# A three-block transformer kernel: unnormalised entry of layer 1, one pass for both norms between the blocks, a shorter gate series, values behind the first scores, elementwise work moved from GpSimd to VectorE

## The chip, the cores and the metric

One core of one Trainium2 chip runs the whole program. The metric is the device time of an execution in microseconds. Engines: TensorE (PE, with PEld for its weight loads), VectorE (DVE), ScalarE (ACT), GpSimd (POOL), SyncE (SP, which issues nearly all DMAs).

## The reference, cut to what matters

Two models in a row on 256 latent tokens of width 1024, each beside a context stream of 256 tokens; float32 throughout. Block 1 is an mLSTM with window attention and a convolutional feed-forward. The second model has layer 0 (retention and a state-space mixer) and layer 1 (latent attention with 16 heads), each with a gated feed-forward.

```
x = first_block(...)                                   # ends with rmsnorm(x, final_norm)
for i in range(2):                                     # second_block: h_lat starts as x, h_ctx is its own context
    a_ctx = rms_norm(h_ctx) * (1 + m_ctx[1]) + m_ctx[0]
    a_lat = rms_norm(h_lat) * (1 + m_lat[1]) + m_lat[0]
    o_ctx, o_lat = retention_ssd_mixer(...) if i == 0 else mla_mixer(...)
    h_lat = h_lat + m_lat[2] * o_lat
    h_lat = h_lat + m_lat[5] * swiglu(rms_norm(h_lat) * (1 + m_lat[4]) + m_lat[3])
    ...                                                # h_ctx the same way, in layer 0 only
return rms_norm(h_lat, final_norm_w)

# mla_mixer: c_q, c_kv, k_pe = split(h @ w_in)   (768, 256, 32 columns)
#   q = rms_norm(c_q) @ w_uq;  k_nope, v = split(rms_norm(c_kv) @ w_ukv)
#   keys and values of context and latent together, softmax over 512 keys, then w_out
# gates: log_sigmoid and softplus, both through log1p(exp(-|x|))
```

The m vectors are products of a conditioning vector with the modulation matrices w_ada.

## The kernel before, in words

Activations lie feature-major: 8 tiles of 128 features by 256 tokens (`xs` latent, `cs` context). Each float32 matmul is three passes (`mm3`, L283 to L287) over a rounded high half and a low half of both operands. `load_w` (L259) brings weights by DMA into tag `wr`, rounds them on ScalarE into `wh` (L270), and takes the low half `wl` by a subtraction (L273). The rule `PW` (L30) puts that subtraction on GpSimd for lane `f` and, in layer 0's latent pass, for the second half of each load of lane `m`; elsewhere on VectorE. A lane is a set of buffers: `m` (main) has 5 PSUM banks and 3 raw weight buffers, `f` (fill) 2 banks and 2 raw buffers, `a` (side) one bank; `L.on(other)` borrows another lane's banks.

The program is written as Python generators, woven with `weave`. The order in which they issue is only a priority: the whole program is one list, scheduled by the tile framework with its own model of times, and `soon()` raises a part's priority. Each engine then runs its instructions in the fixed order which that schedule gave.

Order of the work: modulation and norms; block 1 (projections, gates, mLSTM, window attention, output projection, feed-forward woven with `ada_dve`, which forms modulation columns on VectorE, L417); `final_norm` (L826), which normalises `xs`; layer 0 (`l0_stream`) first for the context on lane `f` up to its states, then for the latents on lane `m`, which begins with a norm of its own (L1124); the feed-forward of both streams, 512 columns wide, woven with more `ada_dve`; layer 1 (`l1`, L1567); the last feed-forward; the last norm.

Two forms of a norm exist. `norm_mod` (L501) squares on ScalarE (`sumsq`), adds on VectorE, sums over features by matmuls with ones (L463), takes the power -1/2 on GpSimd (L229), spreads the result over partitions by a matmul with the identity (L472), and then scales each block on VectorE (L516) and splits it into halves; odd blocks take the low half on GpSimd (L519, L523). The raw form (`raw_mod`, L476) writes unnormalised blocks with two extra columns for the shift as each block of an output projection is finished; matmuls run on 258 columns, and `raw_fix` (L492) applies 1/rms to the result. Before the change only layer 1's feed-forward uses the raw form.

In layer 1, `kv(0)` projects the context to keys and rope part, `kv(1)` the latents, then come 6 query blocks (`ev_q`); `nq` is the norm of the queries, woven with `l1_keys` (keys) and two `proj_tm` (`values`); then the query projection `wuq`, then `attend`, which issues the scores and softmax of 3 heads ahead (`AH1`). In `softmax` (L1008) the first half of the probabilities is scaled on VectorE (L1031), the second on GpSimd (L1032). Further GpSimd work: the first product of `rope` (L577), low halves of the feed-forward activations (L627, L678), and in layer 0 small gated sums (L1318, L1347, L1368, L1387, L1426 to L1428), which the change leaves there.

```
def load_w(self, L, src, n, unit):
    raw = self.tile([P, 1024], F32, "wr" + L.w.name, L.raw)
    nc.sync.dma_start(raw[:, :n], src)
...
    nc.scalar.copy(hi[:, :c1 - c0], raw[:, c0:c1])
    eng = nc.gpsimd if PW(self, L, len(subs)) else nc.vector
    eng.tensor_sub(lo[:, :c1 - c0], raw[:, c0:c1], hi[:, :c1 - c0])
```

## Time and profile before

| | |
|---|---|
| median of 3 runs | 1576.56 us (1572.23 to 1579.45) |
| profiled execution | 1574.25 us, of it 1572.5 us span |
| instructions | 28299, of them 10518 matmuls |
| mean granted TensorE clock | 0.977 of full speed |
| HBM read | 265.60 MB |

The span is what the profile shows between its first and last instruction; the profiled execution is 1.75 us longer. Matmul records are pipelined and their ends modelled, so a busy TensorE can still run below its pace; the number of matmuls in a stretch tells more. A clock of 1.00 is 2.4 GHz, the lower level 0.50 is 1.2 GHz, and a value between is a mean over the stretch. VectorE's busy time holds whatever an instruction spends waiting for memory.

### The profile page before, as it was taken

The numbers are of one execution on the slowest core, as the hardware profiler recorded it, in microseconds if no ns is written. First come the engines' busy times: TensorE is split into PE (matmuls) and PEld (weight loads), VectorE is DVE, ScalarE is ACT, GpSimd is POOL, SyncE is SP. The second block draws the span as 40 slices with busy tenths as digits, with TensorE's granted clock in tenths as the row PEclk, the third lists the DMA queues.
The fourth block names the chain that finished last, engine by engine and source line by source line (L and its number), as shares of the span: only waits on it lengthen the run. The fifth ranks groups of instructions, "written<-read, shape, count | busy, mean of one in ns | idle before, by whom it ended". The sixth has DMA issues, their size and how long they took to land.

```text
span 1572.5 us, 28299 instructions
## 1 busy us (share of the span) xinstructions
PE 1500.6 (95%) x10518; PEld 1328.4 (84%) x10518; DVE 1141.5 (73%) x2369; ACT 789.3 (50%) x1703; POOL 397.4 (25%) x373
## 2 busy tenths in 40 slices
PE   5899999999999997999899999999998999999997
PEld 3598877889999977889899888888898865899997
DVE  4457588589999946777775347988686776687776
ACT  3444547575545455644474323322355556566563
POOL 0102136143222254466572101101011112010000
PEclk9799999999999998999999999999999999999999
DMA  9855651347777763424255225688533340255553
GB/s 335 275 183 202 230 186 41 134 175 237 255 251 240 243 209 121 130 91 148 69 168 167 95 88 207 208 290 275 179 122 109 101 139 1 95 175 177 185 181 115
DMA packets 81387, 268.50 MB, mean 171 GB/s; under 512 B 9056, under 2 KB 10720, under 8 KB 80992
## 3 DMA queue, kind: packets, MB, share of 16 engines
q1 hardware_dynamic: 80672, 266.16, 50.7%
q8 instruction: 82, 1.34, 0.3%
q10 hardware_dynamic: 576, 0.52, 0.1%
q14 instruction: 57, 0.47, 0.1%
HBM read 265.60 MB, written 1.05 MB: 170 GB/s over the span
## 4 chain that ended last, share of the span: by engine, by line
PE 82%; DVE 9%; issue 4%; DMA 3%; ACT 1%; POOL 0%; SPq 0%; POOLq 0%; DVEq 0%; ACTq 0%
PE t_ppm L285 18%; PE t_ppm L287 18%; PE t_ppm L286 18%; PE t_ppf L285 4%; PE t_ppf L286 4%; PE t_ppf L287 4%; DVE t_wlm L273 2%; DMA t_wra<-in_wada 2%; PE t_ppm L1649 2%; PE t_ppa L427 2%; PE t_ppm L1050 1%; PE t_ppf L1064 1%; PE t_ppm L972 1%; PE t_ppm L1082 1%; DVE t_junk L417 1%
## 5 line engine op out<-in xcount | busy, mean ns | idle before, releaser
L270 ACT CAST t_whm<-t_wrm 128x512 fp32r<-128x512 f32 (+2 forms) x588 | 346.3, 598 | 402.6 <-PE t_ppm L286 281.8
L273 DVE TENSOR_TENSOR t_wlm<-t_wrm,t_whm 128x512 fp32r<-128x512 f32 (+3 forms) x551 | 406.0, 743 | 151.7 <-ACT t_whm L270 140.7
L285 PE MATMUL t_ppm<-t_g1m,t_whm 128*128 128x256 f32 x952 | 271.8, 290 | 1.3 <-ACT t_g1m L522 0.8
L287 PE MATMUL t_ppm<-t_g1m,t_wlm 128*128 128x256 f32 x952 | 268.7, 287 | 3.3 <-DVE t_wlm L273 3.2
L286 PE MATMUL t_ppm<-t_g1m,t_whm 128*128 128x256 f32 x952 | 269.7, 286 | 0.0
L287 PEld LDWEIGHTS t_ppm<-t_g1m,t_wlm 128*128 128x128 f32 x952 | 181.9, 192 | 7.5 <-DVE t_wlm L273 5.1
L285 PEld LDWEIGHTS t_ppm<-t_g1m,t_whm 128*128 128x128 f32 x952 | 182.0, 193 | 5.9 <-issue 3.1
L286 PEld LDWEIGHTS t_ppm<-t_g1m,t_whm 128*128 128x128 f32 x952 | 183.0, 193 | 2.0 <-issue 1.7
L273 POOL TENSOR_TENSOR t_wlf<-t_wrf,t_whf 128x512 fp32r<-128x512 f32 (+1 forms) x92 | 121.4, 1333 | 168.5 <-ACT t_whf L270 150.3
L286 PE MATMUL t_ppm<-t_h8m,t_whm 128*128 128x512 f32 (+2 forms) x448 | 159.7, 357 | 1.9 <-DVE t_h8m L525 1.9
L285 PE MATMUL t_ppm<-t_h8m,t_whm 128*128 128x512 f32 (+1 forms) x448 | 158.5, 357 | 2.7 <-ACT t_h8m L524 2.7
L417 DVE SCALAR_TENSOR_TENSOR t_junk<-t_wra,t_sc 128x1024 bf16<-128x1024 f32 x120 | 148.7, 1243 | 16.8 <-DMA t_wra<-in_wada 16.0
L287 PE MATMUL t_ppm<-t_h8m,t_wlm 128*128 128x512 f32 (+2 forms) x448 | 159.5, 357 | 0.0
L270 ACT CAST t_whf<-t_wrf 128x512 fp32r<-128x512 f32 (+2 forms) x148 | 82.9, 573 | 99.9 <-PE t_ppf L286 70.6
L286 PE MATMUL t_ppm<-t_part,t_whm 128*128 128x258 f32 (+1 forms) x400 | 114.1, 285 | 0.0
L287 PE MATMUL t_ppm<-t_part,t_wlm 128*128 128x258 f32 (+1 forms) x400 | 113.8, 285 | 0.0
L285 PE MATMUL t_ppm<-t_part,t_whm 128*128 128x258 f32 (+1 forms) x400 | 113.4, 284 | 0.0
L287 PE MATMUL t_ppm<-t_g2m,t_wlm 128*128 128x256 f32 x352 | 98.9, 284 | 0.6 <-DVE t_wlm L273 0.5
L285 PE MATMUL t_ppm<-t_g2m,t_whm 128*128 128x256 f32 x352 | 99.1, 283 | 0.0
L286 PE MATMUL t_ppm<-t_g2m,t_whm 128*128 128x256 f32 x352 | 99.1, 282 | 0.0
L286 PEld LDWEIGHTS t_ppm<-t_h8m,t_whm 128*128 128x128 f32 (+1 forms) x448 | 84.0, 187 | 15.3 <-DVE t_h8m L525 2.3
L285 PEld LDWEIGHTS t_ppm<-t_h8m,t_whm 128*128 128x128 f32 x448 | 83.1, 187 | 16.3 <-ACT t_h8m L524 2.9
(541 smaller groups left out, 3518.3 us busy)
## 6 DMA issues: line engine op xcount, KB each, us to landing
t_wrm<-in_wup SPq DMA_DIRECT2D x132, 512.0 KB, 3.7
t_wra<-in_wada SPq DMA_DIRECT2D x102, 512.0 KB, 4.9
t_wrm<-in_w_fm SPq DMA_DIRECT2D x30, 512.0 KB, 3.6
t_wra<-in_wada20t SPq DMA_DIRECT2D x24, 512.0 KB, 4.4
t_wrf<-in_w_fm SPq DMA_DIRECT2D x20, 512.0 KB, 4.5
t_wrf<-in_wd SPq DMA_DIRECT2D x24, 384.0 KB, 3.8
t_wrm<-in_win_fm SPq DMA_DIRECT2D x17, 512.0 KB, 3.6
t_wrm<-in_wdown SPq DMA_DIRECT2D x16, 512.0 KB, 4.6
```

The lines of the kernel that those rows point to most:

```text
L270: nc.scalar.copy(hi[:, :c1 - c0], raw[:, c0:c1])
L273: eng.tensor_sub(lo[:, :c1 - c0], raw[:, c0:c1], hi[:, :c1 - c0])
L285: mm(ps, ah, bh, start=start, stop=False)
L286: mm(ps, ah, bl, start=False, stop=False)
L287: mm(ps, al, bh, start=False, stop=stop)
L417: nc.vector.scalar_tensor_tensor(self.tile([P, D], BF16, "junk", 1), raw, 1.0, rows[:, c], op0=MUL, op1=MUL, accum_out=out[:, c, i:i + 1])
L427: self.nc.tensor.matmul(ps[32 * c:32 * c + 32, :T], cond[:, 32 * k:32 * (k + 1)], raw[:, c * T:(c + 1) * T], start=k == 0, stop=k == 7, ti ...
L972: nc.tensor.matmul(po[:, d * T:d * T + 129], Wt[d][c][:, sl], vm[c][:, h], start=i == 0, stop=i == len(keys) - 1)
L1050: nc.tensor.transpose(pp[:, j * T + t * P:j * T + (t + 1) * P], Ps[t][:, c * P:(c + 1) * P], self.m["ident"])
L1064: nc.tensor.matmul(po[j * 64:(j + 1) * 64, :T], v[j][c], pt[j][c // 2][:, (c % 2) * T:(c % 2 + 1) * T], start=c == 0, stop=c == 3, tile_po ...
L1082: nc.tensor.matmul(ps, q[:, t * P:(t + 1) * P], kall, start=True, stop=False)
L1649: nc.tensor.matmul(ps, q, K[0:96, hd], start=True, stop=True)
```

## The change

Layer 1: the last down projection of layer 0's feed-forward writes the latents' unnormalised blocks (`raw_mod`, hook `after`), `kv(1)` and the query blocks run on them and are evacuated by `raw_fix`. Between the blocks: `norm_twice` forms the sums of squares of `xs` and of `xs` times the first norm's weight in one pass, gets layer 0's input (`hn`) from both, and normalises `xs` after that. The series for log1p(exp(-|x|)) takes one operation for each term instead of two. The value projections are issued after the first three heads' scores. All weight subtractions, the feed-forward low halves, the odd blocks of `norm_mod`, the product in `rope` and half of the softmax scaling move from GpSimd to VectorE.

```diff
--- before.py
+++ after.py
-PW = lambda k, L, i: L.name == "f" or k.phase == 1 and i == 1
...
@@ log1p_exp_neg_abs
-        nc.vector.tensor_mul(z, e, a)
+        nc.vector.scalar_tensor_tensor(z, e, 2.0, a, op0=MUL, op1=MUL)
         nc.vector.tensor_mul(z2, z, z)
-        nc.vector.tensor_scalar(a, z2, 1.0 / 15, 1.0 / 13, op0=MUL, op1=ADD)
-        for c in (11, 9, 7, 5, 3, 1):
-            nc.vector.tensor_mul(a, a, z2)
-            nc.vector.tensor_scalar(a, a, 1.0 / c, None, op0=ADD)
-        nc.vector.scalar_tensor_tensor(out, z, 2.0, a, op0=MUL, op1=MUL)
+        nc.vector.tensor_scalar(a, z2, 1.0 / (15 * 4 ** 7), None, op0=MUL)
+        for k in range(6, 0, -1):
+            nc.vector.scalar_tensor_tensor(a, a, 1.0 / ((2 * k + 1) * 4 ** k), z2, op0=ADD, op1=MUL)
+        nc.vector.scalar_tensor_tensor(out, a, 1.0, z, op0=ADD, op1=MUL)
@@ load_w
-            eng = nc.gpsimd if PW(self, L, len(subs)) else nc.vector
-            eng.tensor_sub(lo[:, :c1 - c0], raw[:, c0:c1], hi[:, :c1 - c0])
+            nc.vector.tensor_sub(lo[:, :c1 - c0], raw[:, c0:c1], hi[:, :c1 - c0])
@@ sumsq: the squares take an optional per-row factor w
+            nc.scalar.activation(acc, x, AF.Square, scale=scale)
...
+    def norm_twice(self, L, xs, w, a, sh, out):
+        with self.soon():
+            accs = [self.sumsq(L, xs), self.sumsq(L, xs, w)]
+            ps = L.ps()
+            for s, acc in enumerate(accs):
+                for t in range(2):
+                    for i, sq in enumerate(acc):
+                        nc.tensor.matmul(ps[:, 2 * s + t:2 * s + t + 1], sq[:, t * P:(t + 1) * P], self.ones[:, 0:1], ...)
+            v, u, r = L.sm(2), L.sm(2), L.sm(4)
+            nc.vector.tensor_scalar(v, ps[:, 0:2], 1.0 / D, EPS, op0=MUL, op1=ADD)
+            self.rsqrt(L, v, 2, r[:, 0:2])
+            nc.vector.tensor_scalar(u, ps[:, 2:4], 1.0 / D, None, op0=MUL)
+            nc.vector.scalar_tensor_tensor(u, v, EPS, u, op0=MUL, op1=ADD)
+            self.rsqrt(L, u, 2, r[:, 2:4])
...
+            for k in range(8):
+                hi, lo = L.s1(F32R), L.s1(F32R)
+                out.append((hi, lo))
+                t = L.s1()
+                nc.vector.scalar_tensor_tensor(t, xs[k], aw[:, k:k + 1], bcs[0], op0=MUL, op1=MUL)
+                nc.scalar.activation(hi, t, AF.Identity, bias=sh[k])
+                nc.vector.scalar_tensor_tensor(lo, t, sh[k], hi, op0=ADD, op1=SUB)
+        for k in range(8):
+            nc.vector.scalar_tensor_tensor(xs[k], xs[k], w[k], bcs[1], op0=MUL, op1=MUL)
...
@@ norm_mod: no GpSimd, no extra copy for odd blocks
-                return lambda: (nc.gpsimd if k % 2 else nc.vector).tensor_sub(lo, t, hi)
-            if k % 2:
-                nc.scalar.activation(t, t, AF.Identity, bias=sh[k])
-                nc.scalar.copy(hi, t)
-                return lambda: nc.gpsimd.tensor_sub(lo, t, hi)
+                return lambda: nc.vector.tensor_sub(lo, t, hi)
@@ rope
-        nc.gpsimd.tensor_mul(u[:n], q[:n], tab[0][:n])
+        nc.vector.tensor_mul(u[:n], q[:n], tab[0][:n])
@@ ffn and ffn_wide, the same line in both
-                    nc.gpsimd.tensor_sub(lo, y, hi)
+                    nc.vector.tensor_sub(lo, y, hi)
@@ ffn_wide, last down projection of the latent stream: after=raw_mod's hook
+                yield from self.out_proj(L if j else Ld, Wd, y, [streams[j]], nk=f1 - f0, k0=f0,
+                                         after=None if j or i + 1 < len(spec) else after)
@@ block1, its last line
-        self.final_norm(L, xs, "final_norm", xs)
+        self.norm_twice(L, xs, cl(self.col("final_norm", 0, 8)), *mod(), hn)
@@ softmax
-        nc.vector.tensor_scalar(Ps[0], Ps[0], z[:, 0:1], None, op0=MUL)
-        nc.gpsimd.tensor_mul(Ps[1], Ps[1], ap_of(z[:, 1:2], [(0, 512)]))
+        for t in range(2):
+            nc.vector.tensor_scalar(Ps[t], Ps[t], z[:, t:t + 1], None, op0=MUL)
@@ l0_stream
+        h = hn or self.normed(L, xs, *self.mod2(ad, cd, 0))
@@ l1
+        hs = [[(a[:, :T], b[:, :T]) for a, b in h], hr]
+        rx, res = L.s1(), []
         def ev_q(mb, s, ps):
-            cc[mb] = L.s1()
-            nc.scalar.copy(cc[mb], ps[:, :T])
+            cc[mb] = self.raw_fix(L, ps, rx)
...
-        drive(weave(self.norm2(L.on(self.fill), xs, ad, 0, 0, [], half(1)), kv(0)))
+        drive(weave(self.rms_bc(L.on(self.fill), xs, D, res), kv(0)))
+        nc.scalar.copy(rx, res.pop())
...
-        drive(weave(nq, chain(self.l1_keys(L, hk, K), *values)))
+        drive(weave(nq, self.l1_keys(L, hk, K)))
...
-        drive(self.attend(L, first, st, vs, y, 16, AH1, self.fill if PVF else None))
+        att = self.attend(L, first, st, vs, y, 16, AH1, self.fill if PVF else None)
+        for _ in range(AH1):
+            next(att)
+        drive(chain(*values, att))
```

## Rows read from the trace of the kernel before

**Rows 1.** The page's first part: busy us (share of the span) x instructions.

```profile
PE 1500.6 (95%) x10518; PEld 1328.4 (84%) x10518; DVE 1141.5 (73%) x2369; ACT 789.3 (50%) x1703; POOL 397.4 (25%) x373
```

**Rows 2.** Stretches: length, busy time of each engine, clock, DMA share, GB/s.

```profile
340.00:545.00 205.00, 201.64 (x1637) 198.40 (x1636) 204.04 (x351) 107.97 (x211) 53.55 (x41) 0.99 0.75 251
545.00:640.00 95.00, 82.79 (x633) 74.99 (x632) 60.18 (x155) 51.20 (x132) 45.13 (x39) 0.91 0.48 159
640.00:780.00 140.00, 130.96 (x989) 123.66 (x988) 103.47 (x181) 70.05 (x157) 87.30 (x84) 0.99 0.34 108
1180.00:1200.00 20.00, 15.41 (x112) 14.42 (x111) 11.05 (x22) 10.46 (x23) 4.15 (x5) 0.83 0.25 79
1280.00:1300.00 20.00, 17.27 (x69) 8.68 (x67) 15.10 (x42) 13.07 (x34) 7.15 (x6) 0.91 0.19 74
1340.00:1380.00 40.00, 40.00 (x323) 36.98 (x322) 25.49 (x80) 21.90 (x46) 0.70 (x1) 1.00 0.31 101
1360.00:1560.00 200.00, 200.00 (x1662) 200.00 (x1661) 154.85 (x331) 124.00 (x233) 14.95 (x12) 1.00 0.55 174
```

**Rows 3.** TensorE's waits: who waited for whom, total us, times, longest.

```profile
PE t_ppm L1161 <- DVE t_g1m L568: 5.8, 2, 5.0
...
PE t_ppm L285 <- ACT t_h8m L524: 2.7, 1, 2.7
PE t_ppm L1389 <- DVE t_g2m L1386: 2.6, 2, 1.4
PE t_ppm L995 <- DVE t_g1m L994: 2.3, 3, 1.8
...
PE t_ppm L1453 <- DVE t_g1m L1448: 2.2, 2, 1.6
PE t_ppm L1649 <- ACT t_g2m L1022: 2.1, 1, 2.1
```

**Rows 4.** VectorE by line and shape, whole span: busy us, mean ns, idle before.

```profile
L1031 DVE TENSOR_SCALAR t_g2m<-t_g2m,t_smm 128x512 f32<-128x512 f32 x24 | 20.8, 865 | 0.8
L497 DVE TENSOR_TENSOR t_g1m<-t_ppm,t_g1m 128x256 f32<-128x256 f32 x44 | 18.2, 415 | 0.4 <-ACT t_g1m L1662 0.4
...
L484 DVE SCALAR_TENSOR_TENSOR t_part<-t_held,t_part 128x256 fp32r<-128x256 f32 x8 | 3.8, 480 | 0.0
...
L487 DVE TENSOR_TENSOR t_part<-t_held,t_part 128x1 fp32r<-128x1 f32 x16 | 1.8, 154 | 0.0
```

**Rows 5.** VectorE by line and shape, 340 to 545 us.

```profile
L273 DVE TENSOR_TENSOR t_wlm<-t_wrm,t_whm 128x512 fp32r<-128x512 f32 x118 | 97.5, 839 | 1.0 <-ACT t_whm L270 1.0
L417 DVE SCALAR_TENSOR_TENSOR t_junk<-t_wra,t_sc 128x1024 bf16<-128x1024 f32 x53 | 67.4, 1273 | 0.0
...
L600 DVE SCALAR_TENSOR_TENSOR t_held<-t_ppm,t_held 128x256 f32<-128x256 f32 x22 | 10.5, 476 | 0.0
```

**Rows 6.** GpSimd by line and shape, 340 to 545 us.

```profile
L273 POOL TENSOR_TENSOR t_wlf<-t_wrf,t_whf 128x512 fp32r<-128x512 f32 x12 | 20.8, 1740 | 52.0 <-ACT t_whf L270 46.3 <-ACT t_g1m L450 5.0 <-POOL t_g2m L627 0.7
L627 POOL TENSOR_TENSOR t_g2m<-t_g2m 128x512 fp32r<-128x512 f32 x11 | 19.2, 1750 | 65.9 <-ACT t_g2m L626 57.4 <-PE t_ppm L287 8.5
```

**Rows 7.** VectorE in order of time: start us, us, line, operation, out<-in.

```profile
489.94 1.79 DVE L273 TENSOR_TENSOR t_wlm<-t_wrm,t_whm 128x512 fp32r<-128x512 f32 x1
...
491.98 0.68 DVE L273 TENSOR_TENSOR t_wlm<-t_wrm,t_whm 128x512 fp32r<-128x512 f32 x1
...
559.88 3.22 DVE L833 SCALAR_TENSOR_TENSOR t_held<-t_held,t_ppm 128x256 f32<-128x256 f32 x8 [5.57 <-PE t_ppm L472]
...
575.80 0.48 DVE L516 SCALAR_TENSOR_TENSOR t_g1m<-t_held,t_ppm 128x256 f32<-128x256 f32 x1
```

**Rows 8.** TensorE in order of time, around layer 1's values.

```profile
1230.48 0.95 PE L463 MATMUL t_ppa<-t_held,t_g1m 128*128 128x1 f32 x8
...
1235.51 0.39 PE L285 MATMUL t_ppm<-t_whm,t_h2m 128*128 128x512 f32 x1
...
1246.87 0.28 PE L285 MATMUL t_ppm<-t_g1m,t_whm 128*128 128x256 f32 x1
```

More of the change, by code (lines that the diff above doesn't have):

```diff
@@ L24 @@
 NFF = 22
-NKEEP = 5472
+NKEEP = 5480
 AH0 = 1
@@ L449, in sumsq @@
             sq = L.s1()
-            nc.scalar.activation(sq, x, AF.Square)
+            nc.scalar.activation(sq, x, AF.Square, scale=scale)
         return acc, sq
+    def norm_twice(self, L, xs, w, a, sh, out):
+        nc = self.nc
+        with self.soon():
[4 more added lines that the diff above has]
+                    for i, sq in enumerate(acc):
+                        nc.tensor.matmul(ps[:, 2 * s + t:2 * s + t + 1], sq[:, t * P:(t + 1) * P], self.ones[:, 0:1],
+                                         start=i == 0, stop=i == 1)
+            v, u, r = L.sm(2), L.sm(2), L.sm(4)
[4 more added lines that the diff above has]
+            self.rsqrt(L, u, 2, r[:, 2:4])
+            bcs = []
+            for s in (1, 0):
+                bc = L.ps()
+                for t in range(2):
+                    nc.tensor.matmul(bc[:, t * P:(t + 1) * P], ap_of(r[:, 2 * s + t:2 * s + t + 1], [(0, P)]),
+                                     self.m["ident"], start=True, stop=True)
+                bcs.append(bc[:, :T])
+            aw = self.keep(8)
+            nc.vector.tensor_mul(aw, ap_of(a[0], [(1, 8)]), ap_of(w[0], [(1, 8)]))
+            for k in range(8):
[7 more added lines that the diff above has]
+            nc.vector.scalar_tensor_tensor(xs[k], xs[k], w[k], bcs[1], op0=MUL, op1=MUL)
     def rms_bc(self, L, xs, n, res, eps=EPS):
@@ L646, in ffn, with ffn_wide @@
         yield from down(n - 1)
-    def ffn_wide(self, L, Wu, Wd, h, streams, act, spec):
+    def ffn_wide(self, L, Wu, Wd, h, streams, act, spec, after=None):
         nc = self.nc
@@ L710, in swiglu_act, with block1 @@
         return act
-    def block1(self, xs, hc, hx, ad, early, early2, late):
+    def block1(self, xs, hc, hx, ad, early, early2, late, mod, hn):
         nc, L, m = self.nc, self.main, self.m
@@ L1030, in softmax @@
         nc.vector.reciprocal(z, z)
-        nc.vector.tensor_scalar(Ps[0], Ps[0], z[:, 0:1], None, op0=MUL)
-        nc.gpsimd.tensor_mul(Ps[1], Ps[1], ap_of(z[:, 1:2], [(0, 512)]))
+        for t in range(2):
+            nc.vector.tensor_scalar(Ps[t], Ps[t], z[:, t:t + 1], None, op0=MUL)
         return Ps
@@ L1558, in norm2, with ffn2_both @@
         return self.norm_mod(L, xs, *self.mod2(ad, cd, o), out, slots=slots)
-    def ffn2_both(self, L, i, ad, xs, cs, spec):
+    def ffn2_both(self, L, i, ad, xs, cs, spec, after=None):
         h, half = L.halves(8)
@@ L1563, in ffn2_both, with l1 @@
         streams = [(xs, ad[:, 0, 40:48]), (cs, ad[:, 1, 40:48])]
-        yield from self.ffn_wide(L, self.A[f"wup{i}"], self.A[f"wd{i}"], h, streams, self.swiglu_act, spec)
-    def l1(self, xs, cs, ad):
+        yield from self.ffn_wide(L, self.A[f"wup{i}"], self.A[f"wd{i}"], h, streams, self.swiglu_act, spec, after)
+    def l1(self, xs, cs, ad, hr):
         nc, m, A = self.nc, self.m, self.A
@@ L1571, in l1 @@
         h, half = L.halves(8)
-        hs = [[(a[:, j * T:(j + 1) * T], b[:, j * T:(j + 1) * T]) for a, b in h] for j in range(2)]
+        hs = [[(a[:, :T], b[:, :T]) for a, b in h], hr]
         tab = self.rope_tab(L, "rope3")
@@ L1577, in l1 @@
         hq = []
+        rx, res = L.s1(), []
         def ev_q(mb, s, ps):
-            cc[mb] = L.s1()
-            nc.scalar.copy(cc[mb], ps[:, :T])
+            cc[mb] = self.raw_fix(L, ps, rx)
         def kv(j):
             sl = slice(j * T, (j + 1) * T)
-            c = [L.s1() for _ in range(2)]
+            c = [None] * 2
             def ev_kv(mb, s, ps):
+                if j:
+                    c[mb] = self.raw_fix(L, ps, rx)
+                    return
+                c[mb] = L.s1()
                 nc.scalar.copy(c[mb], ps[:, :T])
@@ L1599, in ev_pe @@
                     return spread
-                rest = self.rope(L, ps[:32, :T], m["rope1p"], tab, [(slice(0, 32), pe[:32, sl])])
+                rest = self.rope(L, self.raw_fix(L, ps[:32], rx), m["rope1p"], tab, [(slice(0, 32), pe[:32, sl])])
                 def later():
@@ L1699, in run @@
         two = lambda i: 2
+        hn = []
         def late(behind):
@@ L1727, in run @@
             self.block1(xs, hc, hx, ads[0], lambda: self.ada(A["wada20"], cond2, "b_ada_20", ads[1], (0, 1)),
-                        lambda: self.ada(A["wada1"], cond1, "b_ada", ads[0], range(2, G1)), late)
+                        lambda: self.ada(A["wada1"], cond1, "b_ada", ads[0], range(2, G1)), late,
+                        lambda: self.mod2(ads[1], 0, 0), hn)
         else:
@@ L1751, in run, with after @@
             next(gc)
-            self.phase = 1
-            for _ in self.l0_stream(M, xs, ads[1], 0, keep, {}):
+            for _ in self.l0_stream(M, xs, ads[1], 0, keep, {}, hn=hn):
                 pass
             cs = next(gc)
-            self.phase = 2
-            spec = SPEC
-            drive(weave(self.ffn2_both(M, 0, ads[1], xs, cs, spec),
+            spec, hooks = SPEC, []
+            def after(k):
+                if not hooks:
+                    hooks.append(self.raw_mod(xs, *self.mod2(ads[2], 0, 0), hr))
+                hooks[0](k)
+            drive(weave(self.ffn2_both(M, 0, ads[1], xs, cs, spec, after),
                         chain(pause(ROWP), last()), 3, 2))
```

24 lines of the change are left out of this document (9 added, 15 removed).

## The prediction, made before the changed kernel ran

> **What bounds the kernel now.** I read the page's first part, then a table of stretches with engine busy times and TensorE's granted clock, then who TensorE waited for, then durations by line, and last the order of time at four places. TensorE counts as busy for 95% of the span [rows 1], but its busy time cannot show how full it is, so I count matmuls. In the last feed-forward 1662 matmuls take 200.00 us at clock 1.00, 0.1203 us each [rows 2]: call that the tempo. At it, the 1637 matmuls of 340 to 545 us need 196.9 us (8.1 lost of 205), the 633 of 545 to 640 need 76.2 (18.8 lost, a little less because some are small), the 112 of 1180 to 1200 need 13.5 (6.5 lost). So the kernel is bound by the number of matmuls, which the change leaves nearly as it is, and what can be won is a few scattered losses: waits of 1 to 6 us each [rows 3] and the lower clock level behind them (0.83 mean in 1180 to 1200 is a third of that stretch at 1.2 GHz).
>
> VectorE is the second limit. From 340 to 545 us it is busy 204.04 of 205 [rows 2]: feed-forward of block 1 together with the modulation rows on L417. There GpSimd's work and VectorE's are not independent. The subtraction on L273 takes 0.68 us when GpSimd is quiet and 1.79 us at 489.94, and its mean over the stretch is 0.839 [rows 5, 7]; L600, which reads PSUM, stays at 0.476 [rows 5]. So L273 pays 118 x (0.839 - 0.68) = 18.8 us.
>
> **The change, part by part.** The sum is made against the profiled execution (1574.25 us, of it 1572.5 span); the median shown is 2.3 us above it, which I add at the end.
>
> *A. Layer 1 takes the latent stream unnormalised.* Removed: the wait of the second key/value pass for the normalised blocks, of it 2.7 us behind ScalarE's half [rows 3], and the lower clock after it: these are the 6.5 us lost from 1180 to 1200 [rows 2]. Now the blocks are written as each one of the last down projection ends, and 1/rms is needed first when a result is evacuated; the context pass's 72 matmuls, 8.7 us at the tempo, lie between. The same form already stands before layer 1's feed-forward: through 1340 to 1380 TensorE is at 40.00 of 40 and clock 1.00 [rows 2], so it works without a stall. Added on VectorE: 8 x (0.48 for L484 + 4 x 0.154 for the two bias columns) = 8.8 us beside the last down projection, and 9 evacuations with a product of 0.415 and a copy of about 0.154, 5.1 us [rows 4]; removed there, the latent norm's 12 operations on VectorE and 4 on GpSimd. Two more columns in 258 cost the matmuls nothing: the tempo above is already that of 258-column ones. Ends 0 (the 8.8 us delay weights) and 6.5; I take 5.5, near the row of the stretch.
>
> *B. Both norms between the blocks in one pass.* Before, the first normalisation starts at 559.88 and the second can use its statistics only at 575.80 [rows 7]: 15.9 us in series. Now the latent input of layer 0 is ready about that much earlier; eight more squares go to ScalarE, which has 51.20 busy of 95 [rows 2], and eight one-column matmuls move. The context stream already covers most of the series for TensorE, so the 15.9 us are not the gain. What goes is further on: the waits of L1161 (5.8 us, 5.0 in one piece, on the convolution's VectorE work) at a place where VectorE has everything at once [rows 3]. With the latent projections earlier, that work spreads into a stretch where VectorE is at 60.18 of 95. The shorter gate series belongs here: 8 small operations in place of 14, in 4 places, about 0.17 us each (nearest row: 0.154 for a tiny one), 1 us on one path. The f-lane's subtractions that come to VectorE here fit in the same idle time. Ends 0 (the context work that fills is only used up sooner) and 12 (this wait and the clock, 0.09 of 95 us, less their overlap); I take 5.
>
> *C. No large elementwise work on GpSimd, layer 0.* From 640 to 780 us GpSimd is at 87.30 of 140 [rows 2], and weight subtractions stand in its queue in front of the small gated sums on which the norm waits. They leave; VectorE, at 103.47 of 140, can take them. Waits here are L1389 (2.6) and L1453 (2.2) [rows 3]. Ends 0 and 6 (both, and 0.01 of clock in 140 us); I take 3.
>
> *D. The same, block 1's feed-forward.* Twelve subtractions of L273 (mean 1.740) and 11 of L627 (1.750) move [rows 6]: 23 x 0.68 = 15.6 us, plus one smaller, 16 us, to an engine that is full. Against it stand the 18.8 us that L273 alone pays; GpSimd's 40 us in these two lines are three quarters of its 53.55 there, so 14 us vanish, and some more on lines that also read two operands from SBUF (L417: mean 1.273). That is near nothing in VectorE's load; the fill lane's low halves come in 0.68 instead of 1.74, which is a small gain. Ends: a loss of 16 (no relief) and a gain of 8.1 (all that TensorE loses there); I take +2.
>
> Here a rule bears. The row: an SBUF operation of VectorE beside GpSimd is longer by up to 1.1 us, a PSUM one by nothing. The Trainium skill, "SBUF — State Buffer", section "Who interferes with whom", says that the pair of ports is locked exclusively and that whoever issues first holds it for the whole instruction. By that rule VectorE could win back up to the whole 40 us of these lines rather than 14, D would be the full 8.1, and C and F would reach their ends; I keep the row's figure, and the rule's case is rival 1.
>
> *E. Values behind the first scores.* Removed: TensorE's wait in the first scores (2.1 on L1649, and 0.09 x 20 = 1.8 us of clock from 1280 to 1300) [rows 2, 3]. But those 48 wide matmuls now cover the norm of the queries: its statistics matmul stands at 1230.48 and the first query projection at 1246.87 [rows 8], and the values fill 11.4 us of that. Without them the keys end at about 1235.5, and TensorE waits for the first normalised block; the weight buffers ahead are held by the query projection, so the values can hardly slip in. What waits behind is all of the query projection. Loss 0 to 8 plus a clock step of 2; gain 0 to 4 (the scores themselves wait for PSUM banks that the softmax frees, and the values need four of the same banks). I take -1.5.
>
> *F. Window attention and the mixer of block 1.* GpSimd's half of the probabilities goes to VectorE; L1031, 0.865 mean [rows 4], loses the GpSimd product of L1032 that runs beside it; that product comes to VectorE at no more than the same price, 24 times in the whole kernel, where VectorE has room. L994's product waits (2.3 us) [rows 3] for the same reason. Ends 0 and 3 (the wait, and some of the first); I take 2. The rope products and the feed-forward splits of layers 0 and 1 change nothing: TensorE is full there (200.00 of 200 with VectorE at 154.85 [rows 2]).
>
> Sum: 5.5 + 5 + 3 + 2 - 1.5 + 2 = 16, so 1558.2 for the profiled execution and 1560.5 with the 2.3: **1560 us**.
>
> **Rivals.**
> 1. *GpSimd was holding VectorE far more than I count* (one whole GpSimd instruction per collision). For: 1.79 against 0.68 is almost a whole instruction of GpSimd. Against: most L273 are undisturbed, or the mean would not be 0.839. Then B is 8, C 6, D 8.1, F 3: 5.5 + 8 + 6 + 8.1 - 1.5 + 3 = 29.1, 1547 us.
> 2. *The query norm comes into the open.* E is -10 in place of -1.5, 1568.5 us. For: 11.4 us of cover go and the chain is 16 us long [rows 8]. Against: a matmul or two of that chain waited for its turn and would come earlier.
> 3. *The waits move rather than go*: the one list schedule of the whole kernel is made anew, B to F come to 1 us together, only A stays: 1574.25 - 6.5 + 2.3 = 1570 us. That is also the case in which the change does not do what it says. For: the losses are small and each has another late operand close behind it. Against: A to F lie in different stretches.
> 4. *VectorE becomes the bound, slower.* In block 1's feed-forward it has 1 us of 205 free. If the stretching of L273 is not relieved, 16 us arrive on a full engine, every weight's low half is late, and TensorE waits for them: 1574.25 + 16 - 5.5 + 2.3 = 1587 us. It decides from the point where the relief is under 8 us (half of the added load, given the gain elsewhere). For: the added load is certain, the relief inferred. Against: PSUM-reading lines are not stretched and two-operand SBUF lines are.
>
> **How the numbers follow.** Forecast 0.45, rival 1 0.11, rival 2 0.17, rival 3 0.16, rival 4 0.11. The bound for a real difference is 0.5% (about what a measurement of this kernel can tell from no change), so faster means below 1568.7 and slower above 1584.4. Faster: 0.43 of the forecast, 0.11, half of rival 2, 0.4 of rival 3: 0.69. Slower: rival 4 but for 0.01: 0.10. Same: 0.21. The range holds all but rival 4 and what lies beyond rival 1: 1542 to 1580.
>
> **What would show it.** A: no wait on the layer-1 input and clock 1.00 in that stretch. B: no wait of 5 us on L1161's transposes, first layer-0 matmuls of the latent lane some 15 us earlier. C, D, F: L273's mean near 0.68 and VectorE's total busy time within some 30 us of 1141.5; VectorE busy much above that would be rival 4. E: a new wait ahead of the query projection, none in the scores. The prediction is wrong if the 340 to 545 stretch gets longer, or if the losses reappear after the layer-0 mixer.

## The result, and the profile after

The changed kernel takes 1559.32 us (median of 4 runs, 1557.49 to 1561.69) against 1576.17 (4 runs, 1572.23 to 1579.45): ratio 0.990, 95% interval 0.987 to 0.993. A second measurement of the same kernel gave 1560.21 (ratio 0.989, 0.987 to 0.991). The forecast was 1560. The sum was right, the terms were not: most of the gain came from the moves off GpSimd, which I had given less than half of it.

The profiled execution took 1561.69 us, 12.6 less than the one before. The page's first part of the changed kernel (busy us, share of the span, x instructions), which answers to [rows 1]:

```profile
PE 1498.8 (96%) x10518; PEld 1329.1 (85%) x10518; DVE 1182.0 (76%) x2649; ACT 793.1 (51%) x1673; POOL 81.9 (5%) x113
```

GpSimd lost 315 us of work, and VectorE gained only 40. Its stretches, as in [rows 2]:

```profile
340.00:545.00 205.00, 203.62 (x1667) 200.82 (x1666) 193.36 (x360) 121.20 (x230) 15.76 (x21) 0.99 0.72 240
545.00:640.00 95.00, 88.78 (x687) 81.83 (x687) 80.59 (x209) 51.86 (x129) 6.74 (x6) 0.95 0.51 170
640.00:780.00 140.00, 133.47 (x985) 125.75 (x985) 116.06 (x240) 72.98 (x160) 30.57 (x36) 0.96 0.35 114
1180.00:1200.00 20.00, 18.63 (x153) 17.80 (x154) 12.70 (x31) 13.62 (x24) 1.39 (x2) 1.00 0.36 116
1280.00:1300.00 20.00, 20.00 (x100) 10.40 (x98) 13.21 (x37) 13.12 (x33) 0.00 (x0) 1.00 0.00 1
```

From 340 to 545 us VectorE is busy 193.36 us in place of 204.04 although some 16 us of work came to it; four modulation rows, some 5 us, have left the stretch, and the rest is time that its instructions no longer lose (below). TensorE has 1667 matmuls there in place of 1637. Over the whole trace its granted clock is at the lower level for 58.7 us in place of 73.2, so by an estimate (half of the difference) up to 7 of the 12.6 us are the clock behind the waits. TensorE's waits (who waited for whom, total us, times, longest), as in [rows 3]:

```profile
PE t_ppm L1279 <- ACT t_g2f L1513: 3.4, 1, 3.4
PE t_ppf L1422 <- DVE t_g2f L1419: 2.8, 1, 2.8
PE t_ppf L282 <- DVE t_h8m L558: 2.3, 1, 2.3
...
PE t_ppm L283 <- DVE t_g1m L485: 1.9, 1, 1.9
PE t_ppm L1422 <- DVE t_g2m L1419: 1.6, 1, 1.6
PE t_ppm L281 <- ACT t_g1m L555: 1.4, 3, 1.0
...
PE t_ppm L282 <- DVE t_g1m L556: 0.7, 1, 0.7
```

The 5 us on the convolution's transposes and the wait on layer 1's input are gone; the scores now begin at 1256 us (1276 before), with a wait of 0.7 us (1.7 in a second profile, 2.1 before). New are 2.8 us on L1422, which no step of mine named, 1.9 us for L485, a low half that `norm_twice` itself writes (at 598 us), and 2.1 us in four pieces for the query norm (L555 and L556, from 1223 us on). The 3.4 us on L1279 stand ahead of the latents' gates of layer 0 (2.4 with the norms in series). And VectorE by line and shape from 340 to 545 us, as in [rows 5] (busy us, mean ns):

```profile
L269 DVE TENSOR_TENSOR t_wlm<-t_wrm,t_whm 128x512 fp32r<-128x512 f32 x114 | 79.3, 708 | 3.9 <-ACT t_whm L268 3.1
L413 DVE SCALAR_TENSOR_TENSOR t_junk<-t_wra,t_sc 128x1024 bf16<-128x1024 f32 x49 | 60.5, 1235 | 1.5 <-DMA t_wra<-in_wada1t 1.5
```

Over the whole trace, the scaling of the probabilities (L1031 in [rows 4]), with both halves on VectorE now:

```profile
L1067 DVE TENSOR_SCALAR t_g2m<-t_g2m,t_smm 128x512 f32<-128x512 f32 x48 | 22.7, 515 | 0.6
```

Two readings of the whole trace are used below. **VectorE's stretching**: for each line, operation and size on VectorE, what its durations lie above their own tenth percentile, summed. It is 123 us before and 32 after (24.8 and 4.7 from 360 to 545 us, 41.5 and 11.0 from 545 to 840; worked out from the instruction records). **The lag**: all matmul columns in order of their start, and the time at which a kernel has begun the same share of them as the profiled changed kernel; a step in it shows where time is lost, and the second profile of the same kernel shows how far it can be trusted (up to 2.8 us). In us, at eight times (worked out from the matmul records):

```
                   320    360    520    840   1160   1200   1240   1540
before             4.3   -1.7    1.6   10.4    9.7   14.3    6.5   13.1
same kernel again  0.7   -0.1   -0.9   -1.3   -1.3    0.0   -0.2    0.8
moves alone        1.7    0.5   -1.3   -2.4   -2.9    2.3   -5.5    0.2
weights alone      5.6   -0.3   -3.4   -4.5   -5.3    2.5   -5.4    1.5
moves undone       3.7   -2.1    1.8   15.8   15.8   15.2   15.1   16.3
A undone          -2.3   -3.1   -4.3   -4.1   -4.3    3.0    2.8    3.5
norm undone       -1.5   -1.8   -3.3   -7.7   -7.8   -7.3   -7.5   -4.7
E undone           0.5   -0.6   -1.9   -4.4    1.7    4.8   -2.9    1.3
```

### The profile page after: what moved, and what is told of

It is laid out like the page before. It is cut to its first block, busy times and chain, and to the rows that moved or that the text cites. A ratio compares the mean times of both kernels' runs of the same rounds, so it can differ in the third digit from the quotient of the medians.

```text
span 1559.9 us, 28122 instructions
## 1 busy us (share of the span) xinstructions
PE 1498.8 (96%) x10518; PEld 1329.1 (85%) x10518; DVE 1182.0 (76%) x2649; ACT 793.1 (51%) x1673; POOL 81.9 (5%) x113
## 4 chain that ended last, share of the span: by engine, by line
PE 58%; issue 13%; DVE 4%; ACT 1%; DMA 1%; POOL 0%; POOLq 0%; DVEq 0%; ACTq 0%
PE t_ppm L281 13%; PE t_ppm L283 13%; PE t_ppm L282 13%; PE t_ppf L281 4%; PE t_ppf L282 4%; PE t_ppf L283 4%; PE t_ppm L1688 2%; PE t_ppf L1099 1%; DVE t_wlm L269 1%; PE t_ppm L1085 1%; PE t_ppm L1545 1%; PE t_ppm L1516 0%; DVE t_g1m L592 0%; PE t_ppm L614 0%; DMA t_wra<-in_wada1t 0%
## 5 line engine op out<-in xcount | busy, mean ns | idle before, releaser
L268 ACT CAST t_whm<-t_wrm 128x512 fp32r<-128x512 f32 (+2 forms) x588 | 349.8, 599 | 414.2 <-PE t_ppm L282 340.7
L269 DVE TENSOR_TENSOR t_wlm<-t_wrm,t_whm 128x512 fp32r<-128x512 f32 (+2 forms) x588 | 390.6, 670 | 138.9 <-ACT t_whm L268 130.5
L283 PE MATMUL t_ppm<-t_h8m,t_wlm 128*128 128x512 f32 (+2 forms) x376 | 139.0, 370 | 0.0
L282 PE MATMUL t_ppm<-t_h8m,t_whm 128*128 128x512 f32 (+2 forms) x376 | 137.8, 368 | 0.0
L281 PE MATMUL t_ppm<-t_h8m,t_whm 128*128 128x512 f32 (+2 forms) x376 | 137.6, 368 | 0.0
L283 PE MATMUL t_ppm<-t_part,t_wlm 128*128 128x258 f32 (+2 forms) x472 | 133.7, 284 | 0.0
L281 PE MATMUL t_ppm<-t_part,t_whm 128*128 128x258 f32 (+2 forms) x472 | 133.6, 284 | 0.0
L282 PE MATMUL t_ppm<-t_part,t_whm 128*128 128x258 f32 (+2 forms) x472 | 133.4, 283 | 0.0
L269 DVE TENSOR_TENSOR t_wlf<-t_wrf,t_whf 128x512 fp32r<-128x512 f32 (+2 forms) x148 | 92.7, 635 | 24.7 <-ACT t_whf L268 23.2
L281 PEld LDWEIGHTS t_ppm<-t_part,t_whm 128*128 128x128 f32 (+1 forms) x472 | 89.3, 189 | 0.7 <-issue 0.4
L282 PEld LDWEIGHTS t_ppm<-t_part,t_whm 128*128 128x128 f32 (+1 forms) x472 | 89.0, 189 | 0.3
```

The source lines that it names most:

```text
L269: nc.vector.tensor_sub(lo[:, :c1 - c0], raw[:, c0:c1], hi[:, :c1 - c0])
L281: mm(ps, ah, bh, start=start, stop=False)
L282: mm(ps, ah, bl, start=False, stop=False)
L283: mm(ps, al, bh, start=False, stop=stop)
```

## The experiments

Theory at the start: the terms A to F as predicted. Rivals: each term's gain belongs to another edit, or is given back later. Every kernel was timed in five rounds beside runs of the kernel before, in four series (medians of before 1575.16, 1576.86, 1576.37 and 1577.41). The first four rows are one series, the next four the second, then three, then one.

| run | what | median us | ratio to before, 95% |
|---|---|---|---|
| u_values | changed, E undone | 1565.77 | 0.9937 (0.9918 to 0.9956) |
| u_moves | changed, C, D, F undone | 1580.43 | 1.0024 (1.0007 to 1.0041) |
| u_twice | changed, norms in series again | 1557.97 | 0.9886 (0.9868 to 0.9904) |
| b_raw | before, A alone | 1578.31 | 1.0019 (1.0004 to 1.0034) |
| after_again | changed, unaltered | 1560.21 | 0.9891 (0.9872 to 0.9910) |
| b_moves | before, C, D, F alone | 1561.92 | 0.9908 (0.9891 to 0.9924) |
| u_raw | changed, A undone | 1565.10 | 0.9926 (0.9909 to 0.9943) |
| u_ghost | changed, idle work on GpSimd | 1664.54 | 1.0558 (1.0537 to 1.0578) |
| ut_values | u_twice, E undone | 1565.48 | 0.9931 (0.9910 to 0.9952) |
| t_late4 | u_twice, modulation rows later | 1566.52 | 0.9942 (0.9920 to 0.9965) |
| b_weights | before, weights' subtractions alone | 1563.88 | 0.9918 (0.9900 to 0.9937) |
| t_norm | u_twice, four operations back on GpSimd | 1561.43 | 0.9897 (0.9875 to 0.9919) |

**The moves, undone.**

```diff
-            nc.vector.tensor_sub(lo[:, :c1 - c0], raw[:, c0:c1], hi[:, :c1 - c0])
+            eng = nc.gpsimd if PW(self, L, len(subs)) else nc.vector
+            eng.tensor_sub(lo[:, :c1 - c0], raw[:, c0:c1], hi[:, :c1 - c0])
...
-        nc.vector.tensor_mul(u[:n], q[:n], tab[0][:n])
+        nc.gpsimd.tensor_mul(u[:n], q[:n], tab[0][:n])
```

(and the norms' odd halves, the feed-forwards' splits and half the probabilities)

> The changed kernel with all elementwise work that the change took from GpSimd given back to it (edits C, D and F undone; raw entry, one-pass norms, gate series and values as changed). Theory: the moves are worth 4.1 us up to 320 us, 1.7 in block 1's feed-forward and 3.2 in the mixer of layer 0, and cost the 5 us between 320 and 340 us (TensorE there waits for VectorE's products of the context mixer): 1559.3 + 4 = 1563.3, the loss at 320 to 340 gone, VectorE's busy time back near 1140 us and its stretching (time above the undisturbed duration) back from 32 us to about 120. Rival 'waits move': the gains at those places come from the other edits and the new order, so 1558 to 1560. Rival 'the moves cost': with the 5 us gone, 1554 to 1556.

Measured: 1580.43, 20 to 21 us slower than the changed kernel and slower than before. The stretching came back to 117 us, VectorE's total to 1138.5. Its waits show where it went:

```profile
PE t_ppm L1493 <- DVE t_g1m L1488: 4.5, 1, 4.5
...
PE t_ppm L1201 <- DVE t_g1m L608: 3.1, 1, 3.1
PE t_ppm L1429 <- DVE t_g2m L1426: 3.0, 2, 1.7
```

L1201 is the transposes' line here (L1161 before): 3.1 of its 5 us are back.

The loss at 320 to 360 us did go (lag 3.7 to -2.1), and far more was lost from 520 to 840 (1.8 to 15.8): both rivals fall, and my size of 4 too.

**The moves alone, on the kernel before** (the same edits the other way).

> The kernel before with the GpSimd moves alone (C, D and F, with no other edit). Undoing them in the changed kernel cost 21 us, three times what I gave them. Theory 'the moves carry the change': 1555 to 1560, with VectorE's time above the undisturbed durations down from 123 to about 30 us. Theory of the prediction (7 us in all, minus the 5 us lost at 320 to 340): 1568 to 1573. Rival 'the moves pay only together with the other edits, since these load GpSimd's and VectorE's queues otherwise': 1572 to 1576.

Measured: 1561.92, 14.9 us faster than the kernel before in its series; stretching 31 us. That is nearly the whole effect of the change. The page's first part, then two stretches of it, then the same two of the kernel before:

```profile
PE 1495.3 (96%) x10518; PEld 1326.7 (85%) x10518; DVE 1181.3 (76%) x2629; ACT 791.6 (51%) x1671; POOL 85.0 (5%) x113
```

```profile
360.00:545.00 185.00, 184.68 (x1544) 184.42 (x1543) 177.34 (x328) 107.05 (x205) 11.79 (x15) 1.00 0.74 242
545.00:840.00 295.00, 282.73 (x2179) 268.21 (x2178) 240.92 (x543) 159.90 (x360) 38.83 (x43) 0.97 0.46 144
```

```profile
360.00:545.00 185.00, 181.94 (x1481) 179.54 (x1480) 184.04 (x314) 96.50 (x188) 48.91 (x35) 0.99 0.75 249
545.00:840.00 295.00, 273.75 (x2110) 258.64 (x2109) 206.79 (x409) 159.48 (x372) 169.22 (x154) 0.96 0.41 135
```

TensorE gains 2.7 and 9.0 us of busy time there. Against the kernel before, the lag gives: 2.6 us won up to 320, 4.8 lost to 360, 5.1 won to 520, 9.9 to 840, nothing after.

**The weights' subtractions alone, on the kernel before** (the first edit of the diff above, the other way).

> The kernel before with the subtractions of the weights' low halves alone moved from GpSimd to VectorE (L273: 118 of 512 columns and a few smaller, 162 of the 309 us that leave GpSimd when all is moved, 1561.9). Theory 'the gain follows the load taken from GpSimd': half of 15, 1568 to 1570, VectorE's time above its undisturbed durations from 123 to about 75 us. Theory 'the weights' low halves are what TensorE waits for': 1561 to 1564. Rival 'the operations in the mixers' and norms' chains are': 1573 to 1577.

Measured: 1563.88, 12.5 us faster than the kernel before in its series, five sixths of what all moves give; stretching 72.5 us. Its page's first part:

```profile
PE 1498.6 (96%) x10518; PEld 1327.6 (85%) x10518; DVE 1161.6 (74%) x2498; ACT 791.4 (51%) x1703; POOL 232.0 (15%) x244
```

So half of the load off GpSimd gave most of the gain. That fits the second theory in time. Not in its mechanism: summed over all of TensorE's waits from 60 to 1545 us, those for VectorE are 29.7 us before, 17.7 here, 16.8 with all moves and 14.4 in the changed kernel; those for GpSimd are 0.0, 1.4, 3.6 and 1.4. VectorE's own waits for GpSimd are 12.3, 7.2, 2.7 and 4.0. TensorE had been waiting for VectorE: some 21 of the 29.7 us were for products in the mixers and only 4.5 for low halves of weights, which fell no further than to 3.5. So the time follows TensorE's waits for VectorE (12.0 of the 12.9 us that all moves take off them), not the summed stretching. That the subtractions held VectorE up is argued from this: they were half of GpSimd's moved load and ran all along.

There is another way in which GpSimd could cost time. A raw weight buffer comes free only when its subtraction is done, and in the kernel before SyncE waits long for GpSimd before it can load the next weights:

```profile
SPq L263 <- POOL t_wlf L273: 153.2, 33, 13.3
SPq L263 <- POOL t_wlm L273: 113.8, 33, 18.1
```

Both are gone with the subtractions moved. But if late weights were the loss, TensorE would wait for their halves, and these waits fall by 1.2 us only (4.7 to 3.5, high halves included).

**Work of the same size on GpSimd that nobody reads.**

```diff
             nc.vector.tensor_sub(lo[:, :c1 - c0], raw[:, c0:c1], hi[:, :c1 - c0])
+            if PW(self, L, len(subs)):
+                self.ghost(nc.gpsimd.tensor_sub, hi[:, :c1 - c0], hi[:, :c1 - c0])
```

(and so at the other places of the moves)

> The changed kernel, all work where it puts it, and on GpSimd in addition an operation of the same size at every place from which one was moved (on the high half or on the operand itself, into a scratch tile that nobody reads; nothing waits for it, but the order is planned anew with it). It loads the SBUF ports as before, without delaying any operand by GpSimd's own slowness. Theory 'interference': VectorE's time above the undisturbed durations goes from 32 back to 100 to 130 us and the time to 1572 to 1580. Theory 'latency' (a low half came 1.74 us after its turn in place of 0.68, and behind others in GpSimd's queue): VectorE is stretched as much, but the time stays at 1559 to 1564.

Measured: 1664.54. The stretching is 125 us, as before the change, with no moved operand coming late from GpSimd: VectorE is held by GpSimd's activity as such. The time is no measure of that. The schedule was made anew with this work in it, and it is not true that nothing waits for the idle work: a high half's buffer comes free only when that work has read it, and ScalarE waits 30.3 us for this:

```profile
ACT t_whf L276 <- POOL t_ghost L180: 24.6, 21, 4.6
ACT t_whm L276 <- POOL t_ghost L180: 5.7, 3, 3.8
```

VectorE in order of time (start us, us, operation) shows what dominates:

```profile
515.26 1.21 DVE L423 SCALAR_TENSOR_TENSOR t_junk<-t_wra,t_sc 128x1024 bf16<-128x1024 f32 x1
516.40 0.08 DVE L423 DVE_READ_ACCUMULATOR t_junk<-t_wra,t_sc 128x1 f32 x1
516.40 0.18 DVE L251 SCALAR_TENSOR_TENSOR t_lgf<-t_lgf 128x32 f32<-128x32 f32 x1
516.51 0.42 DVE L615 SCALAR_TENSOR_TENSOR t_g1f<-t_g1f 128x256 f32<-128x256 f32 x1
516.84 1.22 DVE L423 SCALAR_TENSOR_TENSOR t_junk<-t_wra,t_sc 128x1024 bf16<-128x1024 f32 x1
```

Between any two small steps of a gate series stands a modulation row of 1.2 us, and TensorE waits 10.6 us in one piece for what comes behind. How the 15 us divide between the stretching and the later arrival of what GpSimd computed stays open: TensorE's waits for weights' halves allow the second little, but VectorE's own waits for GpSimd (12.3 us before, 2.7 with the moves alone) are of that kind.

**The norms in series again.**

```diff
-        self.norm_twice(L, xs, cl(self.col("final_norm", 0, 8)), *mod(), hn)
+        self.final_norm(L, xs, "final_norm", xs)
```

> The changed kernel with the two norms between the blocks in series again (the norm part of edit B undone; the short gate series stays). Theory: the 6.5 us won between 540 and 640 us are due to the norm: 1564.3 (4 to 6 more), first latent gate matmul of layer 0 some 8 us later, and a wait of several us on the transposes of L1161 of before back. Rival 'the f-lane's subtractions, no longer behind GpSimd, won it': 1559 to 1561, first latent matmul later but no wait. Rival 'all of it is given back later': later at 640 us by 6, and by nothing at 900.

Measured: 1557.97, 1.4 to 2.2 us faster than the changed kernel, within the intervals: the one pass is worth nothing. The first matmul of layer 0's latent gates starts at 624.9 us before, 616.7 with the moves alone, 616.0 in the changed kernel and 612.2 here: the moves brought it forward. Nor is there a wait of 5 us on the convolution's transposes. The gates come behind the projections, though, and the prediction spoke of these. The latents' first projection in layer 0, in the kernel before, in the changed kernel and with the moves undone:

```profile
581.40 0.29 PE L285 MATMUL t_ppm<-t_whm,t_g1m 128*128 128x272 f32 x1
```

```profile
582.63 0.28 PE L281 MATMUL t_ppm<-t_whm,t_g1m 128*128 128x272 f32 x1
```

```profile
573.69 0.29 PE L284 MATMUL t_ppm<-t_whm,t_g1m 128*128 128x272 f32 x1
```

So the one pass brings the projections 8 us forward only while GpSimd has its old work; in the changed kernel they start 1.2 us later than before (581.4 with the norms in series). Why was not followed up. The transposes' wait of 5.0 us is down to 3.1 with the moves undone, to 0.2 in the changed kernel and to nothing here. With the moves alone TensorE waits 2.4 us at this place, put down to a step of the old gate series:

```profile
PE t_ppm L1156 <- DVE t_lgm L245: 2.4, 1, 2.4
```

So the short series may have paid, but it was not tried by itself.

**A alone, and A undone.**

```diff
-        hs = [[(a[:, :T], b[:, :T]) for a, b in h], hr]
+        hs = [[(a[:, j * T:(j + 1) * T], b[:, j * T:(j + 1) * T]) for a, b in h] for j in range(2)]
...
-            cc[mb] = self.raw_fix(L, ps, rx)
+            cc[mb] = L.s1()
+            nc.scalar.copy(cc[mb], ps[:, :T])
```

(the changed kernel with A undone; A alone is the same edits the other way on the kernel before)

> The changed kernel with the raw entry of layer 1 undone (edit A). Theory of the prediction: 5.5 slower than the changed kernel, 1565, with the wait for the normalised blocks (2 to 3 us) and the slower clock back near 1180 us. Rival from the run of A alone on the kernel before, which was 3 us slower: the same or faster, 1555 to 1559. Rival 'half': the waits are back but VectorE is free at the end of layer 0, 1561 to 1563.

> The kernel before with the raw entry of layer 1 alone (edit A). Theory: 1576.2 - 6 = 1570; no wait for the normalised blocks at 1187 to 1193 us, clock 1.00 from 1180 to 1200, nothing given back up to the end. Rival 'given back': ahead by 6 at 1200 us and by under 2 at the end, 1574 to 1576.

Measured: A undone costs 4.9 us (1565.10 against 1560.21 in the same series). From 1160 to 1200 us the lag grows by 7.3 us against 1.3 in the second profile of the changed kernel: 6.0 at the place. The stretch from 1170 to 1190 us with A undone, and in the changed kernel:

```profile
1170.00:1190.00 20.00, 15.43 (x102) 14.02 (x102) 10.96 (x24) 10.31 (x22) 1.68 (x1) 0.74 0.18 55
```

```profile
1170.00:1190.00 20.00, 18.63 (x158) 18.16 (x158) 14.03 (x43) 12.19 (x25) 1.39 (x2) 1.00 0.40 132
```

But A alone on the kernel before is 3.1 us slower. It wins at its place there too: between 1160 and 1200 us the lag of the kernel before grows by 4.6 us and that of A alone not at all (19.7 to 19.4). But from 1080 to 1160 it has grown by 5.9 (13.8 to 19.7), in layer 0's feed-forward, most of it ahead of the matmuls that A changes.

**E undone, twice.**

```diff
-        drive(weave(nq, self.l1_keys(L, hk, K)))
+        drive(weave(nq, chain(self.l1_keys(L, hk, K), *values)))
...
-        for _ in range(AH1):
-            next(att)
-        drive(chain(*values, att))
+        drive(att)
```

> The changed kernel with the value projections woven back under the query norm (edit E undone, all else kept). Theory: in the changed kernel TensorE waits 1.9 us for the query norm with a slower clock behind it and is 6.9 us later there, and gets 4.9 us back in the scores; so undoing E gives about 2 us: 1557.3 us against 1559.3, no gap ahead of the query projection, and the wait of 2 to 4 us in the first scores back. Rival 'the query norm in the open costs more than that' : 1554. Rival 'E gains, since the scores need not wait': 1562 to 1564.

> The changed kernel with the norms in series (as in the run before, 1558.0) and the values woven back under the query norm: edit E tried a second time. In the first try the time was 6.4 us longer, but its trace put the loss at 1100 us, ahead of layer 1, where SyncE waited 22.2 us in 19 pieces for earlier modulation transfers before issuing the next (6.0 us in 5 in the changed kernel). Theory 'E is worth nothing or little, the plan cost the rest': with these waits short 1555 to 1559, with them at 15 us or more some 5 more. Rival 'E itself is worth 6': 1564, and TensorE's lag arises between 1200 and 1300 us.

Measured: 1565.77 and 1565.48, 5.6 to 7.5 us slower than with E, while from 1160 us to the end the lag changes by -0.4 in the first pair and -0.3 in the second. That is a sum of two things. From 1200 us on, where the edit stands, the kernel without E is 3.5 us faster in the first pair and 3.4 in the second; of the other rows of the lag table, those without E gain 1.0 to 2.1 us there, and those with it lose 0.5 to 2.6. So E loses some 3 us at its own place. Between 1160 and 1200 us the kernel without E is 3.1 us slower in both pairs, behind a clock of 0.83 and 0.87 from 1180 to 1200 us (1.00 with E); but a kernel with E, the one with four operations back on GpSimd, has 0.83 there too and loses 3.2, so this part is hardly E's. The large loss is again at 1100 us. SyncE's waits from 840 to 1190 us before it issues a modulation row, with E undone, with A alone on the kernel before, and in the changed kernel:

```profile
SPq L407 <- DMA t_wra<-in_wada: 22.2, 19, 2.6
```

```profile
SPq L411 <- DMA t_wra<-in_wada: 19.1, 18, 3.1
```

```profile
SPq L407 <- DMA t_wra<-in_wada: 6.0, 5, 3.2
```

and TensorE's longest wait from 840 to 1160 us with E undone:

```profile
PE t_ppm L281 <- DVE t_g2m L743: 4.5, 1, 4.5
```

In the second try they are 22.9 us in 19 pieces, and 4.2. Exactly the three kernels that have A while the values are woven under the query norm show this; in the other ten the sum is 0.9 to 7.7 us. The schedule makes SyncE wait for earlier rows to land, VectorE then stands in front of late rows (18.7 to 20.3 us in all three, at most 16.4 in the others), and the feed-forward's gating queues behind. As far as these kernels show, E's whole gain is that it avoids a schedule which A would otherwise bring. Why the scheduler makes that of it was not tried.

**The new loss at 320 to 360 us.** VectorE of the changed kernel in order of time; in brackets the idle time before, and its releaser:

```profile
332.58 1.22 DVE L413 SCALAR_TENSOR_TENSOR t_junk<-t_wra,t_sc 128x1024 bf16<-128x1024 f32 x1 [4.83 <-DMA t_wra<-in_wada1t]
...
334.73 1.27 DVE L269 TENSOR_TENSOR t_wlm<-t_wrm,t_whm 128x512 fp32r<-128x512 f32 x1
335.92 1.21 DVE L413 SCALAR_TENSOR_TENSOR t_junk<-t_wra,t_sc 128x1024 bf16<-128x1024 f32 x1
...
338.00 0.68 DVE L1419 TENSOR_TENSOR t_g2f<-t_held 128x512 f32<-128x512 f32 x1
```

TensorE waits 2.8 us for the last row. I first took the two modulation rows ahead of it for the cause, and then a full VectorE:

```diff
-                    chain(self.ada_dve(self.A["wada1t"], ..., lambda: hb), late(hb)), *A2))
+                    chain(pause(4), self.ada_dve(self.A["wada1t"], ..., lambda: last[-1]), late(hb)), *A2))
```

(`last[-1]` is the newest block of the feed-forward)

> The changed kernel with the norms in series, and the modulation rows in block 1's feed-forward started some 20 us later, behind the first blocks of the feed-forward. In the changed kernel TensorE waits 2.8 us at 335 us for a product of the context mixer that stands in VectorE's queue behind two of these rows (1.2 us each), and it waits 1.6 us just before; with the clock behind it 5 us are lost there. Theory 'the rows' place makes this loss': no such wait, 1553 to 1555. Rival 'VectorE is full up to 545 us, so what is taken out in front is owed at the end': the wait goes and another comes before 560, 1557 to 1560.

```diff
+            if odd and k % 2:
+                nc.scalar.activation(t, t, AF.Identity, bias=sh[k])
+                nc.scalar.copy(hi, t)
+                return lambda: nc.gpsimd.tensor_sub(lo, t, hi)
...
-        h = self.normed(L, xs, cl(af), cl(ad[:, 0, 24:32]))
+        h = self.normed(L, xs, cl(af), cl(ad[:, 0, 24:32]), odd=True)
```

> The changed kernel with the norms in series (1558.0), and in block 1's norm ahead of its feed-forward the four odd low halves back on GpSimd, as before; all else moved. Where only the weights' subtractions had moved, those four stood on GpSimd and the loss at 320 to 360 us did not arise. Theory 'those four operations (4 x 0.48 us, on a VectorE that is full there) make the loss': no wait of 2.8 us near 335 us, and 1553 to 1555, a version that beats both. Rival 'VectorE's queue is full anyway, the wait moves or is owed by 560 us' (as when the rows were put later): 1557 to 1562.

Measured: 1566.52 and 1561.43, both slower than the 1557.97 they started from. With the rows later the wait is gone and the lag at 360 us is 10.2 us ahead of the changed kernel, but by 840 us it is 2.5 behind: TensorE waits for low halves and for the rows that PE itself works on (waits from 320 to 640 us):

```profile
PE t_ppf L283 <- DVE t_wlf L269: 3.4, 4, 2.1
PE t_ppa L423 <- DMA t_wra<-in_wada: 2.8, 1, 2.8
PE t_ppm L283 <- DVE t_wlm L269: 2.5, 4, 1.2
```

With the four operations back on GpSimd, the wait is as it was:

```profile
PE t_ppf L1426 <- DVE t_g2f L1423: 3.1, 2, 2.8
```

Both were read too late from the right row, the first of the changed kernel's above: VectorE is not full there, it stands idle 4.83 us for the transfer of the first modulation row, with all else queued behind. It is 3.8 us with the four operations back and 3.7 with the moves alone, but 0.8 before and 0.9 with the weights alone, where the loss does not arise: in those two the row stands later in VectorE's order. What would follow, letting that transfer start earlier, was not run.

No version beats the changed kernel beyond doubt; the norms in series are 1.4 to 2.2 us faster and simpler.

**The changed kernel again.**

> The changed kernel once more, unaltered, as the measure for the others of this call and for how far one profile may be trusted. Expected 1559.3, all runs within 1556 to 1563. If one profile's places hold, TensorE waits again at 335 us (2.8 us), 613 us (3.5) and 1222 us (1.9), and nowhere near 1100 us; if the transfers' pace differs from execution to execution, a wait of 2 to 5 us appears in the feed-forward of layer 0, where one was seen in the kernel with the values woven back.

Measured: 1560.21 (1555.97 to 1562.36), the same waits at 335, 613 and 1222 us to within 0.3 us, and none near 1100. A place in one profile holds; what differs from run to run is spread.

## Why the prediction came out right, and where it was wrong

- **A, 5.5.** Right in size and place: 4.9 by the medians, 6.0 at the place, clock 1.00 there as I said (0.91 in the second profile). Not seen: alone it makes the kernel slower, by what the new schedule does some 80 us earlier.
- **B, 5: wrong.** The failed step is "What goes is further on: the waits of L1161 ... With the latent projections earlier, that work spreads". The latents' projections are not 15 us earlier but 1.2 us later; the gates behind them are 9 us earlier, and the moves did that. The transposes' wait goes without the one pass too, with the moves and the short gate series. The one pass brought a wait of its own, 1.9 us for L485. Its value is 0, or -1.4 to -2.2; the short gate series was not tried by itself.
- **C 3, D 2, F 2: the mechanism right, the size half.** 14.9 us for the three. The mis-sized term is "14 us vanish, and some more": in D's stretch the stretching fell by 19.6 us (24.8 to 5.2, from 360 to 545), and D came to 5.1 (0.3 with the loss just ahead of it, next point). C is the larger miss: I priced it by the two waits that I saw behind GpSimd's queue, at most 6, and 9.9 came, because VectorE was held 41.5 us in that part and TensorE waited for its products, whichever they were. F came to 2.6 (up to 320 us), and its reading of L1031 was right: its mean falls from 865 to 515 ns, so that all 48 halves of the probabilities now cost VectorE 22.7 us where 24 had cost 20.8. In total 92 us of stretching went with the moves alone. Rival 1 had the mechanism and, with 17.1 for these three, nearly their size; its whole sum of 29.1, with A and B in full, was not reached.
- **The loss at 320 to 360 us**, 4.8, stood in no step. I had looked at what moves to VectorE there, not at which wait for a transfer moves ahead in its queue.
- **E, -1.5.** At its place right in sign and mechanism and too small: some -3 (a wait of 2.1 us for the query norm ahead of the query projection, as said, and a shorter one in the scores, where I had said none). Its effect on the schedule, 6 us the other way, was not in my reach.
- **The rule** weighed under D (the Trainium skill, "SBUF — State Buffer", "Who interferes with whom") says that the port pair which VectorE shares with GpSimd is an exclusive lock. The runs agree that GpSimd's mere activity holds VectorE (125 us with work nobody reads), and that a PSUM-reading line is not held (L600's operation: 0.478 to 0.483 us in every kernel); the whole 40 us of D's lines did not come back, 19.6 did.
- **VectorE's total** rose by 40.5 us, not within 30: 91 us less of stretching, so some 131 us of added work, that of A and B included.
- Of 16.7 us by the medians I had 16, by the wrong split: 7 in place of 14.9 for the moves, 9 in place of about 1.7 for all the rest. That the errors cancel is luck; and the parts do not add up, since undone one by one they come to 20 for the moves, 4.9 for A and 5.6 for E.

## What to carry to other kernels

Where GpSimd and VectorE both work from SBUF, price GpSimd's work by what VectorE's own instructions take above their undisturbed duration, over the whole trace, and look whether TensorE waits for VectorE: a wait that names VectorE may be GpSimd's doing. How much of the stretching turns into time depends on where TensorE waits, not on its sum. With a list schedule made anew for each edit, an edit's effect can lie far from its place; undo it in the changed kernel and do it alone before crediting it, and compare where in the order the lag arises. In an in-order queue look for the instruction that waits for a transfer, before counting what stands behind it.

## What the runs showed of the hardware that was not expected

VectorE's stretching follows GpSimd's activity closely: 123 us with 397 us of GpSimd work, 117 with 390, 125 with 381, 72.5 with 232, 31 to 32 with 82 to 85. Half of the work that the moves take from GpSimd takes away just over half of it, and with that came five sixths of the moves' gain. Two-operand subtractions are not the only ones held: scaling by one value per row, with a single large operand (L1031, 128x512), takes 0.48 us at its shortest and 1.37 at its longest in the kernel before; at 128x128 (L994) it takes 781 ns in the mean before and 279 in the changed kernel.
